# An MLP in fp16 pieces: how the largest magnitudes get to all partitions

## The chip, the cores and the metric

The kernel runs on one core of a Trainium2 chip. The metric is device microseconds of one execution. A core has five engines that work at the same time, each through its own queue in order: TensorE (PE, with its weight loads as PEld), VectorE (DVE), ScalarE (ACT), GpSimd (POOL) and SyncE (SP), which here issues nearly all DMAs. Engines wait for each other by semaphores. [...]

## The reference

The reference is one layer of a streaming encoder on x (1024 tokens by 1024, float32):

```
n    = RMSNorm(x) * norm1_g;  proj = n @ w_in      # columns: group A, group B
y    = concat(RMSNorm(attention_A(proj)), RMSNorm(attention_B(proj)))
h    = x + y @ w_out
n2   = RMSNorm(h) * norm2_g
u    = square(relu(n2 @ w_ff1))                    # 1024 x 4096
h    = h + u @ w_ff2
out  = RMSNorm(h) * final_norm_g
```

The change touches the MLP alone: the products with w_ff1 (1024 x 4096) and w_ff2 (4096 x 1024).

## The kernel before

The attention part takes the first 380 us or so and isn't touched. Behind it come three parts.

**Tail of the output projection (A).** out_proj_b(tb) makes 128 tokens of y @ w_out for group B on TensorE, for tb = 0 to 7; rows2(tb) adds the residual (VectorE, L1207), makes the row's norm and multiplies it in (L1218); first_half and second_half turn the rows by transposes (L172) and make sums of them for the MLP.

**First product (B).** w_ff1 is taken in eight blocks n of 512 columns. Each block is a matrix product in 2 x 2 sub-blocks by a scheme with seven products p instead of eight (Winograd's form of Strassen's), in the order 1, 5, 6, 3, 7, 2, 4. Each operand is the sum or difference of sub-blocks, and is held as two float16 pieces, a high one and a low one; a product of two such operands is three matmuls (mm3, recorded at L169 as all matmuls are). So a product p of a block is 24 matmuls of 128x128 by 128x512, and a block 168. product1(n, p) issues them; the PSUM results are added and kept by ScalarE (k, L1394) and VectorE (L1404), for p=4 also L1401 and L1402; then comes the squared ReLU on ScalarE (L1405, L1406) and, after p=4, four sums on VectorE (L1412 to L1418). put stores the seven operands for the second product in DRAM (ud).

So that float16 holds them, w is scaled by a power of two taken from its largest magnitude. This is the work that the change is about. For block n: load1(n) loads four tiles w (512 KB each); see1(n) reduces each tile to its largest magnitude per partition (VectorE, L1158); Top.send takes the largest of the four columns (L1163), writes this column of 128 numbers to DRAM (L1164), and reads it back as one row broadcast to all 128 partitions (all_w, L1166); scale1(n) reduces that row (topall, L1170), makes the powers of two (L1133 to L1140, L1312) and has ScalarE scale the four tiles in place (L1315). After that prepare1(n, p) makes the operand's sum (T, L1322, VectorE) and its two pieces: the high one on ScalarE (W, L1348), the low one on GpSimd (L1350), for a few on VectorE. It is called two products ahead of product1.

In the loop over (n, p), see1(n+1) is called after product p=6 of block n, and scale1(n+1) after p=7; for blocks 0 and 1 the calls lie in the loop over tb (scale1(0) after rows2(4), scale1(1) after rows2(7)).

**Second product (C and the end).** w_ff2 and u are taken in four groups g of two blocks, again seven products each, so 14 steps of 24 matmuls to a group. u comes back from ud (fetch2, three steps ahead), w by load2w; the operands are prepared by prepare2 (sums Z, L1322; pieces U and V, L1348 to L1352) two steps ahead; add_up adds a product to the accumulators (C, L1624, VectorE). One power of two per group for w (see2, scale2, with the same Top) and one for u (topu, filled at the end of product p=4 in the first product, and scale_of_u). For group g+1, w is loaded in steps 1 to 8 of group g and seen in steps 3 to 10, with the send after the last; scale2(g+1) is called in step 12. For group 0 all this lies in the last two blocks of the first product (scale2(0) after p=7 of block 7). scale_of_u(g) is called after p=5 of block 2g+2, for the last group in step 4 of group 0.

There are 16 such trips through DRAM: eight for w_ff1, four for w_ff2, four for u.

**What sets the order.** TensorE's instructions keep the order of the program text: each is tied to the one before it (pe, L134). The order of the other engines and of SP's DMAs is a planner's: it plays the program through with modelled durations and lets each engine take what its model has as ready, the earlier call first. So an instruction can stand well ahead of where it was written. Once planned, each engine keeps its order, and an instruction that waits holds up all behind it. SP's queue does so too: the read at L1166 waits there for the write at L1164 to land.

[...]

Of the kernel before, what the change touches and what calls it, by code (L numbers as in the profile page):

```python
# [17 lines left out]
P = 128  # L18
# [16 lines left out]
GQ = 2  # L35
# [21 lines left out]
def kernel(  # L57
# [113 lines left out]
    def transpose(*args):  # L171
        pe(nc.tensor.transpose(*args))  # L172
# [973 lines left out]
    class Top:  # L1146
# [10 lines left out]
        def see(self, src):  # L1157
            nc.vector.tensor_reduce(self.column(), flat(src), mybir.AxisListType.X, ALU.max, apply_absolute_value=True)  # L1158

        def send(self):  # L1160
            assert self.count == self.n
            top = small.tile([P, 1], F32, tag="top", bufs=3, name=f"top_{self.name}")
            nc.vector.tensor_reduce(top, self.cols[:, : self.n], mybir.AxisListType.X, ALU.max)  # L1163
            nc.sync.dma_start(tops[self.slot].rearrange("a p -> p a"), top)  # L1164
            self.all = small.tile([P, P], F32, tag="all", bufs=1, name=f"all_{self.name}")
            nc.sync.dma_start(self.all, tops[self.slot][0].partition_broadcast(P))  # L1166

# [132 lines left out]
    def see1(n, blocks=((0, 0), (0, 1), (1, 0), (1, 1))):  # L1300
        if n not in top1:
            top1[n] = Top(f"w1_{n}", n, 4)
        for b in blocks:
            top1[n].see(w1s[(n, *b)])
        if top1[n].count == 4:
            top1[n].send()

    def scale1(n):
        e = top1.pop(n).bits()
        up1 = power(scale_tile("up1", str(n), 2), e, -1.0, 254 + W_UP)  # L1310
        down1[n] = power(scale_tile("down1", str(n), 3), e, 1.0, -W_UP)
        nc.vector.tensor_tensor(down1[n], down1[n], xdown, ALU.mult)  # L1312
        for b in ((0, 0), (0, 1), (1, 1), (1, 0)):
            w = w1s[(n, *b)]
            nc.scalar.activation(w, w, AF.Copy, scale=up1)  # L1315
# [53 lines left out]
    def product1(n, p):  # L1369
        a, c = chains.setdefault(n, [None, None])  # L1370
        if p in (1, 5, 2):
            ps = pair_psum(f"f1_{n}_{p}")
            if p == 1:
                chains[n][0] = ps
            if p == 5:
                chains[n][1] = ps
        else:
            ps = c if p == 3 else a
        hi, lo = wops.pop((n, p))
        for u in range(2):  # L1380
            cols = slice(u * P, (u + 1) * P)
            for k in range(4):
                x2 = [X[p][k // 2][:, hl, k % 2] for hl in range(2)]
                mm3(ps[:, u], (hi[:, k, cols], lo[:, k, cols]), x2, k == 0 and p in (1, 5, 2), k == 3, True)
                if k % 2:
                    turn()
        kept = saved.setdefault(n, {})
        ps = flat(ps)
        if p in (1, 5, 6):
            if p == 5 and n:  # L1390
                kept[p] = tst([P, 2 * HALF], f"k{n}_{p}")
            else:
                kept[p] = page2([P, 2 * HALF], f"k{n}_{p}")
            nc.scalar.activation(kept[p], ps, AF.Copy)  # L1394
            return
        v = tst([P, 2 * HALF], f"v{n}") if p == 4 else kept[{3: 6, 7: 5, 2: 1}[p]]
        if n not in topf:
            topf[n] = small.tile([P, 4], F32, tag="topf", bufs=2, name=f"topf_{n}")
        top = topf[n][:, {3: 0, 7: 1, 2: 2, 4: 3}[p] :][:, :1]
        if p == 4:  # L1400
            nc.scalar.activation(v, ps, AF.Relu, scale=down1[n])  # L1401
            dve.tensor_reduce(top, ps, mybir.AxisListType.X, ALU.max)  # L1402
        else:
            dve.tensor_tensor_reduce(v, ps, v, 1.0, 0.0, ALU.add, ALU.max, top)  # L1404
            nc.scalar.activation(v, v, AF.Relu, scale=down1[n])  # L1405
        nc.scalar.activation(v, v, AF.Square)  # L1406
        if p != 4:
            put(n, {3: 2, 7: 4, 2: 1}[p], v)
            return

        u00, u01, u11, u10 = kept[1], kept[6], kept[5], v
        dve.tensor_tensor(u11, u10, u11, ALU.add)  # L1412
        put(n, 5, u11)
        dve.tensor_tensor(u10, u00, u10, ALU.subtract)
        put(n, 7, u10)
        dve.tensor_tensor(u00, u11, u00, ALU.subtract)
        put(n, 6, u00)
        dve.tensor_tensor(u01, u01, u00, ALU.subtract)  # L1418
        put(n, 3, u01)
        if n % GQ == 0:  # L1420
            topu[n // GQ] = Top(f"u{n // GQ}", NQ + n // GQ, GQ)
        top, col = topf.pop(n), topu[n // GQ].column()
        nc.vector.tensor_reduce(col, top, mybir.AxisListType.X, ALU.max)
        nc.vector.tensor_tensor(col, col, down1.pop(n), ALU.mult)
        if n % GQ == GQ - 1:
            topu[n // GQ].send()

    topf, topu = {}, {}

# [81 lines left out]
    def see2(g, tiles):  # L1511
        if g not in top2:
            top2[g] = Top(f"w2_{g}", NQ + NQ // GQ + g, 4 * GQ)
        for tile2 in tiles:
            top2[g].see(w2s[tile2])
        if top2[g].count == 4 * GQ:
            top2[g].send()

    def scale_of_u(g):
        e = topu.pop(g).bits(-10)  # L1520
        uup[g] = power(scale_tile("uup", str(g), 4), e, -2.0, 381 + U_UP)
        udown[g] = power(scale_tile("udown", str(g), 4), e, 2.0, -127 - U_UP)

    def scale2(g):
        e = top2.pop(g).bits(-30)
        up2[g] = power(scale_tile("up2", str(g), 2), e, -1.0, 254 + W_UP)
        down2[g] = power(scale_tile("down2", str(g), 2), e, 1.0, -W_UP)
        nc.vector.tensor_tensor(down2[g], down2[g], udown[g], ALU.mult)
# [17 lines left out]
    for at, (n, p) in enumerate(order1):  # L1546
        if p == (1 if n > 1 else 5) and n:
            load1(n + 1)
        ahead1 = at + (AHEAD1 + 1 if at < AT_ONCE else AHEAD1)

        behind = (n, p) == (0, 2)
        if ahead1 < len(order1) and not behind:
            prepare1(*order1[ahead1], ahead1)
        product1(n, p)
        for work in chores.get((n, p), ()):
            combined(*work)
            if behind and work[0] == 5:
                prepare1(*order1[ahead1], ahead1)
        if 0 < n < NQ - 1:
            if p == 6:  # L1560
                see1(n + 1)
            if p == 7:
                scale1(n + 1)
        if p == 5 and n and n % GQ == 0:
            scale_of_u(n // GQ - 1)
        if (n, p) in ((NQ - 2, 4), (NQ - 1, 1)):
            for tile2 in blocks2(0)[(p == 1) * 4 :][:4]:
                load2w(*tile2)
        if n == NQ - 1:
            if p in (5, 6):  # L1570
                see2(0, blocks2(0)[(p == 6) * 4 :][:4])
            if p == 6:
                for i in range(LOAD2):
                    fetch2(i)
            if p == 7:
                scale2(0)
            if p in (7, 2):
                prepare2({7: 0, 2: 1}[p])
# [113 lines left out]
    for at, (g, p, n) in enumerate(order2[:-GQ]):  # L1692
        fetch2(at + LOAD2)
        step = at % (7 * GQ)
        if g + 1 < NQ // GQ:
            if step in range(1, 9):
                load2w(*blocks2(g + 1)[step - 1])
            if step in range(3, 11):
                see2(g + 1, blocks2(g + 1)[step - 3 :][:1])
            if step == 12:  # L1700
                scale2(g + 1)
        if g + 1 == NQ // GQ and step == 0:
            down, up = down2[g], scale_tile("up", "", 1)
            nc.vector.reciprocal(up, down)
        if (g, step) == (0, 4):
            scale_of_u(NQ // GQ - 1)
        prepare2(at + AHEAD2)
        if at in (0, 1, 3, 5):
            load_acc(*into[{0: 1, 1: 5, 3: 6, 5: 4}[at]])
        if at == 6:  # L1710
            nc.sync.dma_start(gfb, final_g.partition_broadcast(P))
        if product2(g, p, n):
            for q2 in range(2):
                add_up(p, q2)
        if (g, p) == (NQ // GQ - 1, 3) and n % GQ == GQ - 1:
            gains.append(fps.tile([P, D], F32, tag=f"{'ab'[1 ^ g % 2]}0", bufs=1, name="gains"))
            nc.scalar.activation(gains[0], gfb, AF.Copy)
        if (g, p) == (NQ // GQ - 1, 7):
            if n % GQ == GQ - 1:
                h = acc[1, 0, 1][:, 1]  # L1720
                nc.vector.scalar_tensor_tensor(h, banks["a"][1][:, 1], down, h, ALU.mult, ALU.add)
            two = [final(2 * (n % GQ) + b, dve, nc.scalar) for b in range(2)]
            for _ in range(4):
                for work in two:
                    next(work)
# [106 lines left out]
```

## Time and profile before

| | |
|---|---|
| median of 3 runs | 1148.94 us (1145.35 to 1149.75) |
| the profiled execution: its time | 1152.16 us |
| the profiled execution: its span | 1150.1 us |
| TensorE busy, share of the span | 89% |
| VectorE | 67% |
| ScalarE | 57% |
| GpSimd | 35% |

The span runs from the first to the last instruction of the profiled execution; its time has a little more around it. Idle time of an engine costs nothing by itself: what counts is which wait ends last in a stage. In a row of the timeline stand start, duration, engine, line, operation and tiles, and in brackets the idle time before it with what ended it. In the waits stand, after the colon, the total in us, how often, and the longest. In the table of stretches, each engine has its busy us and its number of instructions; PEclk is the clock that TensorE was granted, as a share of the full one.

### The profile page before, as it was taken

The page shows a single profiled execution, that of the slowest core. Times are in us where ns is not written, and L with a number is a line of the kernel's source. Part 1 is how long each engine was busy: PE and PEld are TensorE (multiplying, and loading weights), DVE is VectorE, ACT ScalarE, POOL GpSimd, SP SyncE. Part 2 cuts the span into 40 slices and gives each one's busy share as a digit, 9 for nine tenths or more (in the row PEclk, how much of TensorE's full clock was granted, in tenths as well). Part 3 has the DMA queues.
Part 4 walks back from the last instruction along what each step waited for, and adds up shares of the span by engine and source line. Part 5 has one row for each costly group of instructions (what it writes and reads, how often), then busy time and mean ns, then how long its engine had stood idle before and what let it go on. Part 6 is the DMA issues. An engine that isn't in the chain of part 4 may idle for free.

```text
span 1150.1 us, 13982 instructions
## 1 busy us (share of the span) xinstructions
PE 1025.8 (89%) x4803; PEld 598.2 (52%) x4803; DVE 766.8 (67%) x1299; ACT 656.9 (57%) x1033; POOL 403.9 (35%) x327
## 2 busy tenths in 40 slices
PE   9999999999799785997987797969879979799997
PEld 7788878676567564443433343424324433344443
DVE  6577788776774455955564345326978968697976
ACT  8576676675767275755265355364734535356436
POOL 0566664334546231053344134233113014016023
PEclk9999999999899977998988989989989989999999
DMA  9843559999999531133443333455999345551003
GB/s 359 241 119 86 140 134 201 206 228 214 233 245 226 187 126 60 38 129 148 119 160 137 98 138 117 144 203 139 346 269 325 116 132 166 109 172 67 1 1 147
DMA packets 146183, 184.84 MB, mean 161 GB/s; under 512 B 80576, under 2 KB 100032, under 8 KB 146112
## 3 DMA queue, kind: packets, MB, share of 16 engines
q1 hardware_dynamic: 145968, 183.69, 55.5%
q8 instruction: 38, 0.62, 0.2%
q14 instruction: 33, 0.27, 0.1%
q10 hardware_dynamic: 144, 0.26, 0.1%
HBM read 104.21 MB, written 43.00 MB: 128 GB/s over the span
## 4 chain that ended last, share of the span: by engine, by line
PE 25%; DMA 22%; DVE 15%; issue 6%; ACT 6%; POOL 1%; SPq 0%; DVEq 0%; ACTq 0%; POOLq 0%
PE f L169 9%; DMA top<-top_w 5%; PE f_a L169 4%; DMA all_w<-top 4%; PE op_A L169 4%; DVE tops_w L1158 3%; DMA top<-top_u 3%; DMA w<-in_w_ff_dram 3%; PE f_c L169 3%; DMA u<-ud 3%; PE f_b L169 2%; DVE V L1352 2%; DVE C L1624 2%; ACT w L1315 2%; DVE Z L1322 1%
## 5 line engine op out<-in xcount | busy, mean ns | idle before, releaser
L169 PE MATMUL f<-X,W 128*128 128x512 f16 x1344 | 308.5, 394 | 47.4 <-DVE topf L1404 26.9
L169 PEld LDWEIGHTS <-W 128*128 128x128 f16 x1344 | 135.3, 101 | 219.6 <-issue 69.3
L169 PEld LDWEIGHTS <-U 128*128 128x128 f16 x1356 | 133.6, 99 | 194.7 <-issue 31.8
L169 PE MATMUL f_a<-V,U 128*128 128x512 f16 x756 | 169.7, 385 | 16.6 <-DVE C L1624 14.3
L1350 POOL TENSOR_TENSOR U<-u,U 128x1024 f16<-128x1024 f32 x32 | 76.2, 2388 | 244.0 <-ACT U L1348 200.9
L1350 POOL TENSOR_TENSOR W<-T,W 128x1024 f16<-128x1024 f32 x29 | 68.5, 2375 | 205.3 <-ACT W L1348 192.1
L169 PE MATMUL f_c<-V,U 128*128 128x512 f16 x384 | 87.6, 390 | 10.7 <-DVE C L1624 5.4
L1158 DVE TENSOR_REDUCE tops_w<-w 128x1 f32<-128x1024 f32 x64 | 75.9, 1212 | 29.2 <-DMA w<-in_w_ff_dram 29.1
L1346 ACT ACTIVATE u<-u,uup 128x1024 f32<-128x1024 f32 x32 | 36.4, 1144 | 59.0 <-DMA u<-ud 59.0
L1350 POOL TENSOR_TENSOR W<-w,W 128x1024 f16<-128x1024 f32 x23 | 52.2, 2271 | 46.5 <-ACT W L1348 46.5
L169 PE MATMUL op_A<-w_o,y 128*128 128x512 f32 x192 | 58.7, 433 | 8.3 <-DVE ts_vB L430 5.0
L617 ACT ACTIVATE P_B<-P_B,nm_B 128x640 f32<-128x640 f32 (+2 forms) x64 | 44.2, 691 | 29.7 <-DVE nm_B L614 15.3
L169 PE MATMUL op_B<-w_o,y 128*128 128x512 f32 x192 | 50.3, 417 | 10.5 <-DVE w_n L187 10.3
L1315 ACT ACTIVATE w<-w,up 128x1024 f32<-128x1024 f32 x32 | 34.1, 1136 | 44.5 <-DVE down L1140 43.3
L862 DVE SCALAR_TENSOR_TENSOR H_B<-P_B,rc_B,H_B 128x640 f16<-128x640 f32 (+2 forms) x64 | 51.7, 836 | 10.4 <-ACT H_B L857 10.2
L1348 ACT ACTIVATE V<-Z,up 128x1024 f16<-128x1024 f32 x32 | 36.4, 1139 | 33.2 <-DVE Z L1322 30.2
L169 PE MATMUL ip_qB<-nT,w_qB 128*128 128x512 f32 x192 | 53.8, 406 | 1.1 <-DVE t_kB L404 1.1
L169 PE MATMUL ip_kB<-nT,w_kB 128*128 128x512 f32 x192 | 53.7, 404 | 0.0
L1170 DVE TENSOR_REDUCE topall_w<-all_w 128x1 f32<-128x128 f32 x12 | 3.4, 286 | 73.9 <-DMA all_w<-top 73.9
L1394 ACT ACTIVATE k<-f 128x1024 f32<-128x1024 f32 x24 | 24.5, 1019 | 47.4 <-PE f L169 45.1
L169 PE MATMUL ip_vB<-nT,w_vB 128*128 128x512 f32 x192 | 51.2, 400 | 0.0
L1348 ACT ACTIVATE W<-T 128x1024 f16<-128x1024 f32 x32 | 33.4, 1049 | 31.2 <-DVE T L1322 27.4
(269 smaller groups left out, 2027.1 us busy)
## 6 DMA issues: line engine op xcount, KB each, us to landing
w<-in_w_ff_dram SPq DMA_DIRECT2D x64, 512.0 KB, 6.5
u<-ud SPq DMA_DIRECT2D x56, 512.0 KB, 6.1
ud<-k SPq DMA_DIRECT2D x48, 512.0 KB, 3.0
KkB<-t_kB SPq DMA_DIRECT2D x32, 256.0 KB, 5.1
xr<-in_x_dram SPq DMA_DIRECT2D x8, 512.0 KB, 8.8
st_o<-in_w_out_dram SPq DMA_DIRECT2D x8, 512.0 KB, 5.4
h<-in_x_dram SPq DMA_DIRECT2D x8, 512.0 KB, 4.8
hB<-h SPq DMA_DIRECT2D x8, 512.0 KB, 3.1
```

The source lines that it names most:

```text
L169: pe(nc.tensor.matmul(*args, **kw))
L617: nc.scalar.activation(pr, pr, AF.Exp, bias=nm, scale=-1.0, accum_out=sm)
L862: nc.vector.scalar_tensor_tensor(lo, q, rc, hi, ALU.mult, ALU.subtract)
L1158: nc.vector.tensor_reduce(self.column(), flat(src), mybir.AxisListType.X, ALU.max, apply_absolute_value=True)
L1315: nc.scalar.activation(w, w, AF.Copy, scale=up1)
L1322: engine.tensor_tensor(t, a, b, op)
L1346: nc.scalar.activation(full, full, AF.Copy, scale=up)
L1348: nc.scalar.activation(w[0], full, AF.Copy, scale=1.0 if up is None else up)
L1350: engine.tensor_tensor(w[1], full, w[0], ALU.subtract)
L1352: engine.scalar_tensor_tensor(w[1], full, up, w[0], ALU.mult, ALU.subtract)
L1394: nc.scalar.activation(kept[p], ps, AF.Copy)
L1624: nc.vector.scalar_tensor_tensor(flat(c), flat(ps), down2[g], flat(c), ALU.mult, ALU.add)
```

## The change

Top.send is cut into pieces. gather makes the column of 128 maxima as before. For the first product, spread turns that column, broadcast along the free axis, by one transpose on TensorE into a PSUM tile (tag tp), in which each partition has all 128 maxima; the reduce at L1170 then reads PSUM. This holds for all eight blocks of w_ff1, for u of groups 0 to 2, and for w_ff2 of group 0. The transpose is issued in scale1, scale_of_u and scale2, and so stands in TensorE's order at the place of these calls. For w_ff2 of groups 1 to 3 and for u of the last group, the trip through DRAM stays, but gather, write, read and use are separate calls. With it some calls move: see1(n+1) from p=6 to p=3, the product after it; scale2(0) from p=7 to p=3; load2w and see2 one step earlier, write in step 9, read in step 10, scale2(g+1) in step 12 as before; for the last u, write in step 1, read in step 2, use in step 5 of group 0.

```diff
@@ class Top
-        def send(self):
+        def gather(self):
             assert self.count == self.n
-            top = small.tile([P, 1], F32, tag="top", bufs=3, name=f"top_{self.name}")
-            nc.vector.tensor_reduce(top, self.cols[:, : self.n], mybir.AxisListType.X, ALU.max)
-            nc.sync.dma_start(tops[self.slot].rearrange("a p -> p a"), top)
+            self.top = small.tile([P, 1], F32, tag="top", bufs=3, name=f"top_{self.name}")
+            nc.vector.tensor_reduce(self.top, self.cols[:, : self.n], mybir.AxisListType.X, ALU.max)
+
+        def spread(self):
+            self.all = mps.tile([P, P], F32, tag="tp", bufs=2, name=f"all_{self.name}")
+            transpose(self.all, self.top.to_broadcast([P, P]), ident)
+
+        def write(self):
+            nc.sync.dma_start(tops[self.slot].rearrange("a p -> p a"), self.top)
+
+        def read(self):
             self.all = small.tile([P, P], F32, tag="all", bufs=1, name=f"all_{self.name}")
             nc.sync.dma_start(self.all, tops[self.slot][0].partition_broadcast(P))
@@ see1, product1, see2: send() becomes gather()
@@ scale1
     def scale1(n):
+        top1[n].spread()
         e = top1.pop(n).bits()
@@ scale_of_u, scale2
-    def scale_of_u(g):
+    def scale_of_u(g, spread=True):
+        if spread:
+            topu[g].spread()
         e = topu.pop(g).bits(-10)
...
     def scale2(g):
+        if g == 0:
+            top2[g].spread()
         e = top2.pop(g).bits(-30)
@@ the loop over the first product
         if 0 < n < NQ - 1:
-            if p == 6:
+            if p == 3:
                 see1(n + 1)
...
-            if p == 7:
+            if p == 3:
                 scale2(0)
@@ the loop over the second product
-            if step in range(1, 9):
-                load2w(*blocks2(g + 1)[step - 1])
-            if step in range(3, 11):
-                see2(g + 1, blocks2(g + 1)[step - 3 :][:1])
+            if step in range(8):
+                load2w(*blocks2(g + 1)[step])
+            if step in range(2, 10):
+                see2(g + 1, blocks2(g + 1)[step - 2 :][:1])
+            if step in (9, 10):
+                (top2[g + 1].write if step == 9 else top2[g + 1].read)()
             if step == 12:
                 scale2(g + 1)
...
-        if (g, step) == (0, 4):
-            scale_of_u(NQ // GQ - 1)
+        if g == 0 and step in (1, 2, 5):
+            last = NQ // GQ - 1
+            {1: topu[last].write, 2: topu[last].read, 5: lambda: scale_of_u(last, False)}[step]()
```

More of the change, by code (lines that the diff above doesn't have):

```diff
@@ L1305, in see1 @@
         if top1[n].count == 4:
-            top1[n].send()
+            top1[n].gather()
     def scale1(n):
+        top1[n].spread()
         e = top1.pop(n).bits()
@@ L1425, in product1 @@
         if n % GQ == GQ - 1:
-            topu[n // GQ].send()
+            topu[n // GQ].gather()
     topf, topu = {}, {}
@@ L1516, in see2 @@
         if top2[g].count == 4 * GQ:
-            top2[g].send()
-    def scale_of_u(g):
+            top2[g].gather()
+    def scale_of_u(g, spread=True):
+        if spread:
+            topu[g].spread()
         e = topu.pop(g).bits(-10)
```

## The prediction

> **What bounds the kernel now.** I read the page's shares first, then a table of stretches, then the waits, then single stalls in the timeline.
>
> ```profile
> span 1150.1 us, 13982 instructions
> PE 1025.8 (89%) x4803; PEld 598.2 (52%) x4803; DVE 766.8 (67%) x1299; ACT 656.9 (57%) x1033; POOL 403.9 (35%) x327
> ```
>
> TensorE is busy for most of the span, so the question is what its idle time is worth and where it lies. The table splits the span from the end of the output projection on: projection tail (A), first product (B), second product in two stretches (C), and a stretch for comparison.
>
> ```profile
> core 0: us, PE busy (x) PEld busy (x) DVE busy (x) ACT busy (x) POOL busy (x), PEclk, DMA share, GB/s
> 380.00:458.40 78.40, 52.88 (x240) 42.85 (x239) 39.56 (x89) 40.59 (x64) 15.73 (x14) 0.82 0.29 104
> 458.40:815.60 357.20, 309.83 (x1362) 137.06 (x1360) 195.40 (x273) 188.35 (x196) 119.87 (x52) 0.92 0.42 138
> 815.60:860.00 44.40, 36.12 (x153) 15.48 (x152) 36.56 (x37) 19.50 (x19) 5.33 (x2) 0.92 0.95 289
> 860.00:1010.00 150.00, 130.52 (x580) 56.96 (x578) 119.14 (x111) 70.39 (x67) 32.93 (x14) 0.95 0.58 173
> 1010.00:1102.00 92.00, 92.00 (x428) 41.66 (x426) 76.49 (x59) 48.13 (x46) 29.20 (x12) 1.00 0.20 69
> ```
>
> In the last row TensorE has no idle time and its full clock. Above it TensorE idles 25.5 us in A, 47.4 in B and 27.8 in C, and runs at a clock of 0.82 to 0.95. What it waits for stands in the waits; the second fence has the DMA queue's own.
>
> ```profile
> DVE topall_w L1170 <- DMA all_w<-top: 73.9, 12, 11.0
> ...
> DVE topall_u L1170 <- DMA all_u<-top: 41.6, 4, 11.4
> ...
> PE f L169 <- DVE topf L1404: 26.9, 5, 7.2
> ...
> PE f L169 <- ACT k L1394: 18.5, 2, 9.9
> ```
> ```profile
> SPq L1166 <- DMA top<-top_w: 56.8, 9, 7.4
> ...
> SPq L1166 <- DMA top<-top_u: 25.3, 4, 6.7
> ```
>
> VectorE stands still 115.5 us in 16 waits, each for the maximum's way through DRAM. TensorE never waits for that itself; it waits for VectorE and ScalarE work that is queued behind it. One stall (block n=4 of the first product) shows the chain, VectorE, ScalarE, GpSimd, TensorE:
>
> ```profile
> 653.36 0.29 DVE L1170 TENSOR_REDUCE topall_u<-all_u 128x1 f32<-128x128 f32 x1 [11.23 <-DMA all_u<-top]
> ...
> 656.74 0.28 DVE L1170 TENSOR_REDUCE topall_w<-all_w 128x1 f32<-128x128 f32 x1 [2.47 <-DMA all_w<-top]
> ```
> ```profile
> 657.68 4.27 ACT L1315 ACTIVATE w<-w,up 128x1024 f32<-128x1024 f32 x4 [12.59 <-DVE down L1140]
> 661.85 1.00 ACT L1394 ACTIVATE k<-f 128x1024 f32<-128x1024 f32 x1
> ```
> ```profile
> 663.93 2.13 POOL L1350 TENSOR_TENSOR W<-T,W 128x1024 f16<-128x1024 f32 x1 [17.51 <-ACT W L1348]
> 666.01 2.13 POOL L1350 TENSOR_TENSOR W<-w,W 128x1024 f16<-128x1024 f32 x1
> ```
> ```profile
> 662.90 49.65 PE L169 MATMUL f<-X,W 128*128 128x512 f16 x216 [8.51 <-ACT k L1394]
> ```
>
> VectorE idles 13.7 us for two trips, the scaling of w (L1315) starts only then, ScalarE's copy of a finished PSUM pair (k, L1394) is queued behind it, and TensorE idles 8.51 us for that PSUM pair.
>
> **The change, part by part.** The unit is the full-rate matmul, and the other prices are these:
>
> ```profile
> 1018.38 10.52 PE L169 MATMUL f_a<-V,U 128*128 128x512 f16 x48
> 1028.74 10.52 PE L169 MATMUL f_c<-V,U 128*128 128x512 f16 x48
> ```
> ```profile
> 24.08 0.60 PE L172 MATMUL r<-ident,r 128*128 128x128 f32 x4
> ...
> 407.44 0.41 PE L172 MATMUL tp<-ident,n 128*128 128x128 f32 x1
> ...
> 808.85 6.93 PE L169 MATMUL f<-X,W 128*128 128x512 f16 x24 [2.97 <-DVE topf L1404]
> ```
>
> From start to start 48 matmuls take 10.36 us, 0.216 each. After a gap of 2.97 us, 24 matmuls took 6.93 us where 5.18 is full rate: a gap costs itself and about 1.75 more. I use that for the clock lost per gap.
>
> *Spreading by TensorE (12 of the 16 maxima: 8 of w1, 3 of u, 1 of w2).* Added per maximum: one 128x128 transpose of a broadcast column. Four such cost 0.60 us, a lone one 0.41, so 0.15 to 0.41; I take 0.3, or 3.6 us in all, straight on TensorE, 0.6 of it in A and 3.0 in B. VectorE's reduce then reads PSUM in place of SBUF; I take the same 0.29. Removed: 24 small DMAs, and 12 of the queue's waits at L1166, during which everything behind them on SP (stores of k, loads of w and u) stood too. SP is not what TensorE waits for in A and B, so I book that at nothing; without that cover it is part of the range.
>
> *A, scale1(0) and scale1(1).*
>
> ```profile
> 400.81 0.29 DVE L1170 TENSOR_REDUCE topall_w<-all_w 128x1 f32<-128x128 f32 x1 [8.12 <-DMA all_w<-top]
> ...
> 446.33 0.28 DVE L1170 TENSOR_REDUCE topall_w<-all_w 128x1 f32<-128x128 f32 x1 [8.79 <-DMA all_w<-top]
> ```
> ```profile
> 404.75 2.90 PE L169 MATMUL op_B<-w_o,y 128*128 128x512 f32 x6 [10.32 <-DVE w_n L187]
> ...
> 455.74 1.12 PE L172 MATMUL tp<-ident,n 128*128 128x128 f32 x4 [12.22 <-ACT F L1263]
> ```
>
> Both large gaps of A end only after VectorE's two waits of 8.12 and 8.79. The new transposes stand behind out_proj_b(4) and out_proj_b(7) in TensorE's order, so VectorE has the rows' work (L1207, L1218) to do before them and waits for no trip. Gain: 8.1 + 8.8 = 16.9, plus two clocks of 1.75, less 0.6: 20. Bounds: 16 (no clock) to 28 (all 25.5 of idle, and clock).
>
> *B, six spreads in steady state and the three of u.* B holds 56 products of 24 matmuls; at full rate these 1344 are 1344 x 10.36 / 48 = 290.1 us; B takes 357.2, so 67.1 lie above it. What stays or comes: the 18 old transposes (1362 less 1344), 3; the new ones, 3; then two new dependences.
>
> First, TensorE now waits for the gathered column itself, and behind it in its strict order stand all later matmuls. The column was ready here (VectorE), against TensorE's place (product p=5 of n=2 ends 48 matmuls after 542.01, at 552.4):
>
> ```profile
> 519.51 0.15 DVE L1163 TENSOR_REDUCE top_w<-tops_w 128x1 f32<-128x4 f32 x1
> ...
> 545.80 1.22 DVE L1158 TENSOR_REDUCE tops_w<-w 128x1 f32<-128x1024 f32 x1 [4.16 <-DMA w<-in_w_ff_dram]
> ...
> 554.73 0.14 DVE L1163 TENSOR_REDUCE top_u<-tops_u 128x1 f32<-128x2 f32 x1
> ```
> ```profile
> 532.57 6.83 PE L169 MATMUL f<-X,W 128*128 128x512 f16 x24 [3.83 <-DVE topf L1404]
> ...
> 542.01 32.51 PE L169 MATMUL f<-X,W 128*128 128x512 f16 x142 [1.60 <-POOL W L1350]
> ```
>
> The first column of u would come 2.3 us late; that of w for n=2 comes early, since TensorE stopped at 528.7 after p=2, so p=7 ended near 523.5, 3.9 later. I book 3 us for the three of u and none for w.
>
> Second, scale1(n+1) can no longer start before p=7 of n has ended, and two products (10.4 us) later TensorE needs W(n+1, 1). In the stall shown the chain from the reduce (656.74) to the end of GpSimd's W<-w (668.14) takes 11.4. Ahead of W<-w in it stand W<-T (2.1 on GpSimd) and the copy of k (1.0), late there only because of the stall; without them it is 8.3, and with the transposes' 0.4 and one VectorE pass over 1024 columns before it (1.22, as at 545.80), 9.9: just hidden. Bounds: hidden, or 11.4 + 1.6 - 10.4 = 2.6 us idle per block. I take 1.0 x 7 blocks, 7, by the lower end, because nothing else should hold T back once VectorE runs; clock left over, 3. B gains 67.1 - 3 - 3 - 3 - 7 - 3 = 48; bounds 26 (2.6 x 7 idle with 1.75 x 7 of clock, and the rest) and 60.
>
> [...] The trace has the clock already lost after 2.97 us, so I keep a share.
>
> *C, see2 and load2w a step earlier, write, read and use apart.* Four trips stay (w2 of groups 1 to 3, the last u). VectorE's waits in C:
>
> ```profile
> 852.87 0.29 DVE L1170 TENSOR_REDUCE topall_u<-all_u 128x1 f32<-128x128 f32 x1 [7.77 <-DMA all_u<-top]
> ...
> 911.78 0.15 DVE L1163 TENSOR_REDUCE top_w<-tops_w 128x1 f32<-128x8 f32 x1
> ...
> 924.49 0.29 DVE L1170 TENSOR_REDUCE topall_w<-all_w 128x1 f32<-128x128 f32 x1 [6.65 <-DMA all_w<-top]
> ...
> 999.84 0.29 DVE L1170 TENSOR_REDUCE topall_w<-all_w 128x1 f32<-128x128 f32 x1 [7.52 <-DMA all_w<-top]
> ```
>
> A step is one product, 5.2 us. Gather to use was two steps (10.4), against a trip of 12.7 (911.78 to 924.49); now three (15.5), with SP's wait for the write moved behind a step's loads of u and w; the last u is written after one step, read after two and used after five instead of four. So a trip as measured is hidden, if the planner keeps to the written places: VectorE and SP are planned, and a read that the plan takes for ready can be drawn forward as before. The bound from the other engine: VectorE is busy 155.7 us in C's 194.4, and 733 matmuls need 158.2, so it can hardly fall below some 165. The three waits shown are worth up to 21.9 (the fourth trip was hidden behind other VectorE work); with the clock after three gaps, 5, up to 27. At worst, SP's queue moved past by earlier loads costs 5. I take half of the 27: 14.
>
> [...]
>
> Sum: 20 + 48 + 14 = 82. The profiled execution took 1152.16 us, 2.1 around its span and 3.2 above the median shown; taken off the median, 1148.9 - 82 = 1067.
>
> **Rivals.** *Everything hides*: A 28, B 58, C 24 give 1039. For it: each stall shown ends in one trip. Against: VectorE near its limit in C. *The trips of C still stall*, the planner having drawn them forward: 1067 + 14 = 1081. For it: the waits of 6.65 and 7.52 stood where two steps were written between. *The chain behind p=7 is the new bound*: 2.6 us and 1.75 of clock more per block take B to 26, and C's half goes with it when VectorE is late: 1149 - 20 - 26 - 3 = 1100. For it: 11.4 was measured; against: two of its parts came from the stall. *TensorE's own wait decides, slower*: a spread stands in strict order behind columns that wait for loads of w (4.16 us for one, four in a row for a block). It decides from 82 / 12 = 6.8 us per spread; at 8 us each, with 1.75 of clock, 117 come and 82 go: 1184. Against: the one late column above is late by 2.3. *Little comes of it* (the stalls pass to stores and loads on SP): 1130 to 1149.
>
> **How the numbers follow.** Forecast (1052 to 1076) 0.38; everything hides 0.17; trips of C still stall 0.13; chain 0.20; TensorE's wait, slower, 0.06; little 0.06, half of it within 0.5% (5.7 us, about what a measurement of this kernel can tell from no change). So faster 0.91, same 0.03, slower 0.06. The range goes from 1036 (all upper bounds but a little of C) to 1116 (the lower bounds 16 and 26, and a loss of some 9 in C).
>
> **What would show it.** VectorE's waits for all_w and all_u four, not sixteen; in A no gap of TensorE over 5 us and a clock above 0.9; in B, TensorE's waits on L1404 and L1394 (45.4 us) below 10, its idle time instead in front of the transposes or of W<-w; in C, VectorE's waits at L1170 below 11. It is wrong where the transposes themselves carry waits of 5 us and more, where B stays above 330 us, or where C does not shorten.

## The result and the profile after

The changed kernel takes 1087.68 us (median of 4 runs, 1085.46 to 1088.87); the kernel before, run beside it, 1147.91 (4 runs, 1145.35 to 1149.75). The ratio is 0.9475, with a 95% interval of 0.9449 to 0.95: some 60 us less, where 82 were forecast. The time lies in the range, and 21 us above the predicted one.

The profiled execution took 1085.46 us. The page's shares of the kernel after:

```profile
span 1083.7 us, 13981 instructions
...
PE 1013.8 (94%) x4815; PEld 594.1 (55%) x4815; DVE 790.1 (73%) x1299; ACT 652.2 (60%) x1033; POOL 402.2 (37%) x327
```

The same work of TensorE lies in a span that is 66.4 us shorter (the medians differ by 60.2: the execution that was profiled before lay 4.2 above its median, the one after 2.2 below). The table of stretches of the kernel after, cut at the same places of the work as the prediction's table:

```profile
core 0: us, PE busy (x) PEld busy (x) DVE busy (x) ACT busy (x) POOL busy (x), PEclk, DMA share, GB/s
380.00:433.60 53.60, 48.73 (x237) 39.65 (x236) 39.39 (x79) 31.45 (x53) 14.44 (x12) 0.97 0.37 135
433.60:752.40 318.80, 301.46 (x1371) 135.67 (x1371) 217.70 (x285) 191.66 (x203) 119.52 (x52) 0.98 0.43 152
752.40:796.40 44.00, 38.45 (x168) 16.58 (x166) 40.85 (x41) 20.25 (x20) 5.19 (x2) 0.92 0.91 316
796.40:943.40 147.00, 128.08 (x565) 55.89 (x564) 114.17 (x105) 69.79 (x66) 32.86 (x14) 0.94 0.51 169
```

A fell from 78.4 to 53.6 us and its clock rose from 0.82 to 0.97; B fell from 357.2 to 318.8, clock 0.92 to 0.98. C is what it was: 44.4 and 150.0 us before, 44.0 and 147.0 now, at clocks of 0.92 and 0.95 before, 0.92 and 0.94 now. Measured from the first matmul of op_B (which itself comes 1.1 us earlier) to the first of f, from there to the first of f_a, and from there to the end of the span, the three parts give the span's difference whole:

| us | before | after | gain | forecast |
|---|---|---|---|---|
| up to op_B | 376.0 | 374.9 | 1.1 | 0 |
| A | 82.5 | 58.7 | 23.8 | 20 |
| B | 357.1 | 318.9 | 38.2 | 48 |
| C and the end | 334.5 | 331.2 | 3.3 | 14 |

In the waits of the kernel after, first VectorE's on the trip, then TensorE's in B and C (total, how often, longest):

```profile
DVE topall_w L1178 <- DMA all_w<-top: 18.2, 2, 9.3
```
```profile
PE f_a L169 <- DVE C L1637: 13.6, 5, 7.0
PE all_u L172 <- DVE top_w L1163: 5.7, 2, 2.8
...
PE f_c L169 <- DVE up L1140: 4.2, 1, 4.2
PE all_u L172 <- DVE top_u L1163: 4.0, 1, 4.0
...
PE f L169 <- POOL W L1359: 2.8, 3, 1.2
```

The 45.4 us that TensorE waited in B for topf and k are gone. In their place stand three waits of the new transposes of u (all_u, 9.7 us) and three for W<-w (2.8). In C nothing went away. VectorE's timeline there, with SP's queue, for one of the three trips of w2 left:

```profile
840.57 0.15 DVE L1163 TENSOR_REDUCE top_w<-tops_w 128x1 f32<-128x8 f32 x1
...
853.55 0.29 DVE L1178 TENSOR_REDUCE topall_w<-all_w 128x1 f32<-128x128 f32 x1 [9.31 <-DMA all_w<-top]
...
856.20 1.28 DVE L1637 SCALAR_TENSOR_TENSOR C<-f_a,down,C 128x1024 f32<-128x1024 f32 x1
...
929.47 0.29 DVE L1178 TENSOR_REDUCE topall_w<-all_w 128x1 f32<-128x128 f32 x1 [8.92 <-DMA all_w<-top]
```
```profile
840.75 0.32 SPq L1170 DMA_DIRECT2D top<-top_w  x1
847.80 0.32 SPq L1174 DMA_DIRECT2D all_w<-top  x1
848.21 0.86 SPq L1492 DMA_DIRECT2D u<-ud  x2
```

The read is written a step (5.2 us) behind the write, with that step's loads between; in SP's queue it stands right behind the write, waits 7 us for it to land, and holds the loads of u up. The reduce is written three steps (15.5 us) behind the gather; in VectorE's order three passes stand between, and then it waits 9.31 us of the trip's 13.0. Before, such a wait was 6.65. So both were drawn forward, as the planner does with what its model has as ready.

### The profile page after: what moved, and what is told of

The parts are those of the page before. It is cut to its first block, busy times and chain, and to the rows that moved or that the text cites. A ratio compares the mean times of both kernels' runs of the same rounds, so it can differ in the third digit from the quotient of the medians.

```text
span 1083.7 us, 13981 instructions
## 1 busy us (share of the span) xinstructions
PE 1013.8 (94%) x4815; PEld 594.1 (55%) x4815; DVE 790.1 (73%) x1299; ACT 652.2 (60%) x1033; POOL 402.2 (37%) x327
## 4 chain that ended last, share of the span: by engine, by line
PE 28%; DVE 19%; DMA 9%; ACT 9%; issue 6%; POOL 2%; SPq 0%; DVEq 0%; ACTq 0%; POOLq 0%
PE f L169 9%; PE f_a L169 6%; DMA w<-in_w_ff_dram 4%; PE op_A L169 4%; DVE tops_w L1158 3%; PE f_c L169 3%; DVE V L1361 3%; ACT w L1324 2%; PE op_B L169 2%; PE f_b L169 2%; DVE C L1637 2%; DMA u<-ud 2%; DVE T L1331 2%; DVE Z L1331 1%; DMA top<-top_w 1%
## 5 line engine op out<-in xcount | busy, mean ns | idle before, releaser
L169 PE MATMUL f<-X,W 128*128 128x512 f16 x1344 | 299.3, 385 | 3.5 <-POOL W L1359 2.8
L169 PEld LDWEIGHTS <-W 128*128 128x128 f16 x1344 | 133.0, 99 | 166.0 <-issue 9.8
L1359 POOL TENSOR_TENSOR W<-T,W 128x1024 f16<-128x1024 f32 x29 | 65.4, 2266 | 104.3 <-ACT W L1357 99.7
L1403 ACT ACTIVATE k<-f 128x1024 f32<-128x1024 f32 x24 | 24.4, 1018 | 49.6 <-PE f L169 49.5
L1413 DVE CUSTOM_DVE_ANT_0 k<-f,k 128x1024 f32<-128x1024 f32 x24 | 29.2, 1219 | 34.4 <-PE f L169 34.2
L1414 ACT ACTIVATE k<-k,down 128x1024 f32<-128x1024 f32 x24 | 27.4, 1142 | 41.1 <-DVE topf L1413 41.0
L1357 ACT ACTIVATE U<-u,uup 128x1024 f16<-128x1024 f32 x24 | 27.4, 1141 | 38.8 <-DMA u<-ud 15.5
L169 PE MATMUL ip_qA<-nT,w_qA 128*128 128x512 f32 x192 | 50.2, 395 | 0.3 <-DVE VA L175 0.3
```

The lines of the kernel that those rows point to most:

```text
L169: pe(nc.tensor.matmul(*args, **kw))
L1357: nc.scalar.activation(w[0], full, AF.Copy, scale=1.0 if up is None else up)
L1359: engine.tensor_tensor(w[1], full, w[0], ALU.subtract)
```

## The experiments

The runs were made in two sets, on two chips; the kernel before had a median of 1147.52 us (13 runs) beside the first four kernels, and of 1151.18 (7 runs) beside the others, so kernels of different sets are compared by their ratios to it. The first set holds only_first, only_second, pin_use and u_later, the second dram_pinned, pin_use_read, u_pin and u_pin_see.

### The spreading by TensorE alone (only_first)

The second product's loop is put back; the 12 transposes stay.

```diff
-            if step in range(8):
-                load2w(*blocks2(g + 1)[step])
...
+            if step in range(1, 9):
+                load2w(*blocks2(g + 1)[step - 1])
+            if step in range(3, 11):
+                see2(g + 1, blocks2(g + 1)[step - 3 :][:1])
+            if step == 10:
+                top2[g + 1].write()
+                top2[g + 1].read()
...
+        if (g, step) == (0, 4):
+            scale_of_u(NQ // GQ - 1, False)
```

> The changed kernel with its second product put back: for w_ff2 of groups 1 to 3 load, see and send stand at their old steps, write and read together, and the last u is written and read where it is gathered and used in step 4. Theory (the three steps that lie apart are worth next to nothing, because the plan draws read and use forward in any case): 1088 us, within 5 of the changed kernel, VectorE's waits for all_w and all_u in the second product some 20 us as in both kernels. Rival (the second product gained about what the forecast gave it, and the first product less than thought): 1095 to 1105 us.

Measured: 1090.18 us, ratio 0.9505 (0.9478 to 0.9532), against 0.9475 (0.9449 to 0.95) with both parts. By the spans A is 58.5, B 319.2, C and the end 334.6. So the transposes carry the gain, and the second part adds 3.4 us in C by the spans, an amount that the intervals of the times hardly tell from nothing. VectorE's timeline of this kernel has the same trips in C:

```profile
795.92 0.29 DVE L1178 TENSOR_REDUCE topall_u<-all_u 128x1 f32<-128x128 f32 x1 [7.39 <-DMA all_u<-top]
...
865.54 0.29 DVE L1178 TENSOR_REDUCE topall_w<-all_w 128x1 f32<-128x128 f32 x1 [6.21 <-DMA all_w<-top]
...
939.67 0.29 DVE L1178 TENSOR_REDUCE topall_w<-all_w 128x1 f32<-128x128 f32 x1 [8.16 <-DMA all_w<-top]
```

They come to 21.8 us against 20.9 with the steps apart (2.69 for u, 9.31 and 8.92 for w): what the second part took off the wait for u, it gave back on w.

### The steps apart alone (only_second)

In the first product each spread becomes a write and a read right behind the gather, and see1 and scale2(0) go back to p=6 and p=7; the second product stays as changed.

```diff
             top1[n].gather()
+            top1[n].write()
+            top1[n].read()
...
-        top1[n].spread()
         e = top1.pop(n).bits()
...
-            if p == 3:
+            if p == 6:
                 see1(n + 1)
```

> The kernel before with the second product's part of the change alone: the first product's maxima go through DRAM as before. Theory: the gain belongs to TensorE's spreading, so 1142 to 1150 us, with VectorE's twelve waits of 6 to 11 us back in the first product. Rival (the second product's steps carry 10 to 15 us): 1132 to 1138 us.

Measured: 1145.91 us, ratio 0.9991 (0.9973 to 1.001). Alone, the second part is worth nothing that can be measured. B is 356.6, as before; C with the end is 332.1, about as after; VectorE's waits for the trips are back, 114.1 us in 15.

### The reduce tied behind the last add (pin_use)

If C stalls because the reduce is drawn forward, a tie between two VectorE instructions should be enough: the reduce may stand no earlier in VectorE's order than the add_up last written before it. Trip, DMAs and written places stay.

```diff
-            nc.vector.tensor_reduce(top, self.all, mybir.AxisListType.X, ALU.max)
+            behind_of(nc.vector.tensor_reduce(top, self.all, mybir.AxisListType.X, ALU.max), behind)
...
-        e = topu.pop(g).bits(-10)
+        e = topu.pop(g).bits(-10, last_add[0])
...
-        e = top2.pop(g).bits(-30)
+        e = top2.pop(g).bits(-30, last_add[0])
...
-        nc.vector.scalar_tensor_tensor(flat(c), flat(ps), down2[g], flat(c), ALU.mult, ALU.add)
+        last_add[0] = nc.vector.scalar_tensor_tensor(flat(c), flat(ps), down2[g], flat(c), ALU.mult, ALU.add).ins.name
```

> The changed kernel; in the second product VectorE's reduce of the broadcast maxima is tied, in VectorE's order, behind the last add_up written ahead of it, so that it can't be drawn forward. Theory (the trips of the second product still stall VectorE for 9.3 and 8.9 us since the plan draws the reduce forward): those two waits go below 3 us each, TensorE's gaps of 4.2 and 7.0 us near 857 and 931 go, 1070 to 1078 us. Rival (VectorE is near its limit there, so that another wait takes their place): 1084 to 1092 us.

Measured: 1078.13 us, ratio 0.9402 (0.937 to 0.9433): 9.6 less than the changed kernel, 0.1 above the theory's range and well below the rival's. C and the end fall from 331.2 to 322.1; A and B stay (58.3 and 318.6). VectorE's timeline has two of the reduces, each with its gather ahead of it:

```profile
798.80 0.15 DVE L1169 TENSOR_REDUCE top_w<-tops_w 128x1 f32<-128x8 f32 x1
...
828.76 2.47 DVE L1644 SCALAR_TENSOR_TENSOR C<-f_b,down,C 128x1024 f32<-128x1024 f32 x2
831.14 0.28 DVE L1184 TENSOR_REDUCE topall_w<-all_w 128x1 f32<-128x128 f32 x1
...
848.19 0.14 DVE L1169 TENSOR_REDUCE top_w<-tops_w 128x1 f32<-128x8 f32 x1
...
906.50 2.47 DVE L1644 SCALAR_TENSOR_TENSOR C<-f_b,down,C 128x1024 f32<-128x1024 f32 x2
908.88 0.28 DVE L1184 TENSOR_REDUCE topall_w<-all_w 128x1 f32<-128x128 f32 x1
```

Neither waits; VectorE has no wait for a trip left. So the place of the use in VectorE's order was what failed. The three written steps (15.5 us) are not what hides the trip here: the gather is still drawn forward while its use no longer is, and 32.3 and 60.7 us lie between the two. Without VectorE's 20.9 us of waits TensorE's idle time in C falls from 31.6 to 24.4 us, and its busy time from 299.7 to 297.8 (the mean granted clock of the whole execution is 0.981 against 0.975); 17.4 us of what is left are waits for the adds to C.

### The read's place on SP too (pin_use_read)

As pin_use, and the read on SP is tied behind the load of u last written before it.

```diff
-            nc.sync.dma_start(self.all, tops[self.slot][0].partition_broadcast(P))
+            behind_of(nc.sync.dma_start(self.all, tops[self.slot][0].partition_broadcast(P)), last_fetch[0])
...
-        nc.sync.dma_start(u2s[n, p], ud[n][p - 1])
+        last_fetch[0] = nc.sync.dma_start(u2s[n, p], ud[n][p - 1]).ins.name
```

> pin_use, with the read of the row in SP's queue tied behind the load of u issued last before it, so that fewer loads of u stand behind SP's wait for the write to land. Theory (once VectorE no longer waits, SP's 7 us in front of the read don't reach TensorE): within 3 us of pin_use. Rival (the loads of u behind the read are what is left of the stall): 4 to 8 us below pin_use.

Measured: 1078.22 us, ratio 0.9365 (0.9335 to 0.9395) against 0.9402 (0.937 to 0.9433), spans 1074.0 against 1073.0, C and the end 321.9 against 322.1. But the tie moved nothing. SP's queue at the same trip, first in pin_use, then with the tie:

```profile
848.36 0.32 SPq L1176 DMA_DIRECT2D top<-top_w  x1
849.55 0.32 SPq L1498 DMA_DIRECT2D u<-ud  x1
856.02 0.32 SPq L1180 DMA_DIRECT2D all_w<-top  x1
```
```profile
850.58 0.32 SPq L1178 DMA_DIRECT2D top<-top_w  x1
851.77 0.32 SPq L1501 DMA_DIRECT2D u<-ud  x1
858.90 0.32 SPq L1182 DMA_DIRECT2D all_w<-top  x1
```

In pin_use a load of u already stood between write and read, and all through C the order of SP's DMAs is the same in both kernels. So this is pin_use once more, on the other chip: it shows that C repeats to 0.2 us, and that the ratios of one order can lie 0.4% apart, some 4 us. Whether the loads of u that stand behind the read cost anything stays open.

### The scale of u one product later (u_later)

The three waits of the all_u transposes are the other loss. In the changed kernel scale_of_u(g) is called at p=5 of the next block; here at p=6, one product (5.2 us) later in TensorE's order. Nothing else differs.

```diff
-        if p == 5 and n and n % GQ == 0:
+        if p == 6 and n and n % GQ == 0:
             scale_of_u(n // GQ - 1)
```

> The changed kernel; scale_of_u of groups 0 to 2, and with it the transpose that TensorE waits in, is called after product p=6 in place of p=5, one product (5.2 us) later. Theory (TensorE waits at the three transposes of u, 2.8, 2.8 and 4.0 us, for a column that is gathered behind a reduce that waits for a load of w; the gaps and the clock after them are lost time): no wait left at these transposes, 1072 to 1078 us. Rival (the wait only moves to the next thing that is late): 1084 to 1090 us.

Measured: 1070.79 us, ratio 0.9332 (0.9305 to 0.936): 16.9 less than the changed kernel, 13.8 by the spans, and below the 1072 to 1078 that the theory gave. B falls from 318.9 to 303.7; C with the end is 331.0 (331.2). A is 60.5 (58.7) here and 58.6 in u_pin below, which has the same edit: a part can differ by some 2 us between two executions. The first of the three in TensorE's timeline, after the change and with the call a product later:

```profile
529.89 0.32 PE L172 MATMUL all_u<-ident,top_u 128*128 128x128 f32 x1 [2.83 <-DVE top_w L1163]
530.05 17.39 PE L169 MATMUL f<-X,W 128*128 128x512 f16 x72
547.28 0.27 PE L172 MATMUL all_w<-ident,top_w 128*128 128x128 f32 x1
547.38 36.46 PE L169 MATMUL f<-X,W 128*128 128x512 f16 x168
...
583.79 10.96 PE L169 MATMUL f<-X,W 128*128 128x512 f16 x50
```
```profile
533.83 0.27 PE L172 MATMUL all_u<-ident,top_u 128*128 128x128 f32 x1
533.94 10.52 PE L169 MATMUL f<-X,W 128*128 128x512 f16 x48
```

The transpose no longer waits, and the 48 matmuls behind it run at full rate (10.36 us from 533.94 to the next transpose at 544.30). (The view puts the wait of 2.83 down to top_w, a column that VectorE gathers right behind top_u, at 529.76; the transpose reads top_u.) After the wait of 2.83, the 72 matmuls from 530.05 to 547.28 took 17.2 us, where full rate is 15.5: 1.7 of clock, beside the wait. Behind the second wait, of 2.83 too, 72 matmuls took 17.2 us again, and behind the third, of 4.00, 17.0. The three places make 9.7 + 1.7 + 1.7 + 1.5 = 14.6; the run gives 15.2.

### Trips through DRAM, but used late (dram_pinned)

How much of the first part is the shorter way, and how much the place of its use? Here all 16 maxima go through DRAM again, written and read right behind the gather, but the reduce is tied behind VectorE's last pass over PSUM written before it (in A, behind the rows' multiplication by the norm). scale_of_u and scale2(0) are called at p=7. Each of the three kinds of maxima of the first product has its own all tile.

```diff
             top1[n].gather()
+            top1[n].write()
+            top1[n].read()
...
-        top1[n].spread()
-        e = top1.pop(n).bits()
+        e = top1.pop(n).bits(-90, last_pass[0])
...
-            dve.tensor_tensor_reduce(v, ps, v, 1.0, 0.0, ALU.add, ALU.max, top)
+            last_pass[0] = dve.tensor_tensor_reduce(v, ps, v, 1.0, 0.0, ALU.add, ALU.max, top).ins.name
```

> The changed kernel with the first product's maxima sent through DRAM again, written and read as soon as they are gathered; VectorE's reduce of the row that comes back is tied, in VectorE's order, behind the last pass of product p=7 (for the two blocks ahead of the loop behind the last row multiply), so that it can't be drawn forward; the scales of u are taken at p=7 as well, that of w_ff2 of group 0 too. Theory A (what cost the time was the place of the reduce in VectorE's order, which the transpose only sets by TensorE's order): the trips lie in the slack of 13 to 30 us between gather and p=7, waits are left where the slack is short (block 2, 4 us, w_ff2 of group 0), 1085 to 1105 us. Theory B (the way over TensorE counts because it is short): the waits of 6 to 11 us stay, 1130 to 1150 us.

Measured: 1101.57 us, ratio 0.956 (0.9537 to 0.9582). A is 60.4 (82.5 before, 58.7 after), B 327.2 (357.1, 318.9), C and the end 334.9. So with the old way through DRAM, 22 of A's 24 us and 30 of B's 38 are there. From its VectorE timeline, and TensorE's:

```profile
518.67 0.29 DVE L1188 TENSOR_REDUCE topall_w<-all_w 128x1 f32<-128x128 f32 x1 [5.49 <-DMA all_w<-top]
...
594.78 1.22 DVE L1166 TENSOR_REDUCE tops_w<-w 128x1 f32<-128x1024 f32 x1 [9.15 <-DMA w<-in_w_ff_dram]
```
```profile
525.76 1.03 PE L169 MATMUL f<-X,W 128*128 128x512 f16 x2 [4.82 <-ACT W L1368]
...
606.55 0.98 PE L169 MATMUL f<-X,W 128*128 128x512 f16 x2 [2.87 <-ACT W L1368]
```

Of the first product's twelve reduces one still waits for its trip (5.49), and TensorE then for W (4.82). Its other waits for trips, 22.0 us in three, lie in C, which isn't tied here. VectorE waits longer for a load of w than in the changed kernel (9.15 us against at most 5.5); SP issued a load of w at 586.26, right behind a read (584.88) that had waited for its write. This kernel has u's scale late too, so for the way itself it is to be set beside u_later: A 60.4 against 60.5, B 327.2 against 303.7. Of the 75 us that u_later has gained in A and B, 52 are there without crossing by TensorE, and 23.5 come with it, all in B. How these divide among the trip that still waits, the loads behind SP's reads and the clock wasn't separated. In A, where see1 is called at the places it had before, the 22 us are the tie's, as far as the edit goes. In B they aren't the tie's alone: see1(n+1) stays at p=3, so that the gather is called earlier than in the kernel before, u's scale is taken at p=7, and the all tiles are separate. No run has the tie there without these.

### Both repairs together (u_pin), and the reduces of w2 tied as well (u_pin_see)

u_pin has the edits of pin_use and u_later.

> pin_use and u_later together. Theory (two stalls in two stages, each with its own cause): the gains add up, 1087.7 - 9.6 - 16.9 = 1061 us. Rival (both take from the same slack): 1066 us or more.

Measured: 1063.36 us, ratio 0.9237 (0.9222 to 0.9251). The two gains, 9.6 and 16.9 off 1087.68, make 1061.2; by the ratios they make 0.9402 + 0.9332 - 0.9475 = 0.9259. So they add, as they lie in different parts: B is 303.6, C and the end 324.9. What then holds TensorE in C is late adds: 17.5 us in eight waits for C. see2's reduces over w2 (1.2 us each, some waiting for their load) are drawn in front of them, so u_pin_see ties those too:

```diff
-            top2[g].see(w2s[tile2])
+            top2[g].see(w2s[tile2], last_add[0])
```

> u_pin, with the reduces of w_ff2's tiles (see2) tied behind the last add_up as well. Theory (at the start of the second product TensorE waits 5 us for add_up of the first products, which stands in VectorE's order behind reduces for the next group that could come later): the gap near the third product goes, 1054 to 1058 us. Rival (VectorE is full there, and the order among its work makes no difference, or the late reduces make the write late): 1060 to 1066 us.

Measured: 1053.61 us, ratio 0.915 (0.9136 to 0.9164), a little below the theory's range, 8.5% below the kernel before and 3.4% below the changed one (0.915 / 0.9475). C and the end fall to 315.0. VectorE's timeline, and TensorE's at the same time:

```profile
803.41 1.28 DVE L1644 SCALAR_TENSOR_TENSOR C<-f_b,down,C 128x1024 f32<-128x1024 f32 x1 [1.02 <-PE f_b L169]
806.00 1.28 DVE L1644 SCALAR_TENSOR_TENSOR C<-f_b,down,C 128x1024 f32<-128x1024 f32 x1 [1.30 <-PE f_b L169]
815.37 0.29 DVE L1184 TENSOR_REDUCE topall_w<-all_w 128x1 f32<-128x128 f32 x1 [8.08 <-DMA all_w<-top]
```
```profile
805.80 10.52 PE L169 MATMUL f_a<-V,U 128*128 128x512 f16 x48
817.51 0.38 PE L169 MATMUL f_a<-V,U 128*128 128x512 f16 x1 [1.19 <-ACT V L1363]
818.86 10.30 PE L169 MATMUL f_a<-V,U 128*128 128x512 f16 x47 [0.97 <-DVE V L1367]
```

VectorE waits for trips again, 16.4 us in three waits, 8.08 of it in this one, against 18.2 in two for w in the changed kernel: now that the gather is held back too, VectorE comes to the reduce 7 to 9 us behind it, and the trips take 15.5, 13.1 and 12.0. But the adds stand ahead of the wait: behind this one TensorE idles 1.19 and 0.97 us, behind the 9.31 of the changed kernel 4.21. What a wait costs is what stands behind it.

## Why the prediction was right, and where not

*The bound.* Right: the gain came from VectorE's waits for the trips and what was queued behind them. dram_pinned makes it sharper than the prediction had it: some two thirds of what u_later gains in A and B (52 of 75 us) can be had with the old way through DRAM, if the reduce stands late in VectorE's order and, in B, the gather is called early. In A that is 22 of the changed kernel's 24 us, so there the transposes gain by the place that they give the reduce, through TensorE's strict order, and hardly by being a shorter way; in B place and way weren't separated further.

*A, 20 forecast, 23.8 measured.* Right, within its bounds of 16 to 28. Both gaps of 10.32 and 12.22 us are gone, and no gap over 2.3 us stays in A; the clock is 0.97. The idle time in the stretch fell from 25.5 to 4.9 us (53.6 less 48.73), by 20.6, where the two waits had been booked at 16.9; what the smaller gaps lost as well was left out of the forecast.

*B, 48 forecast, 38.2 measured.* The mechanism was right, and the terms for what comes in its place were mis-sized. The step that failed is "I book 3 us for the three of u and none for w". None for w held: the longest wait of a transpose of w is 0.21 us. For u the prediction took one column's lateness, 2.3, for the sum of three, without clock. The three columns made TensorE wait 2.83, 2.83 and 4.00 and cost 15 with the clock, as u_later shows. This is the mechanism of the rival "TensorE's own wait decides": VectorE's timeline has the wait for a load of w ahead of the column,

```profile
520.62 1.22 DVE L1158 TENSOR_REDUCE tops_w<-w 128x1 f32<-128x1024 f32 x1 [4.04 <-DMA w<-in_w_ff_dram]
...
529.69 0.14 DVE L1163 TENSOR_REDUCE top_u<-tops_u 128x1 f32<-128x2 f32 x1
```

and TensorE's transpose at 529.89 directly behind it. No run takes that load's wait away by itself, so its share in the lateness is read from the rows. The rival's mechanism struck three spreads, at 5 us each with the clock, not twelve at 8, so it took a part of the gain and not the sign.

Two other terms of B were booked too high and made up some of it. The chain behind p=7, booked 7, cost 2.8: only three of the waits for W<-w are left, of at most 1.2 us, so the rival that put it at 1100 is out. The new transposes, booked at 0.3 each, take 0.15: from 547.38 to 583.79, 168 matmuls and one transpose took 36.41, where 168 at full rate are 36.26.

One term was missing: in front of the last old transposes, near B's start, TensorE now waits 2.24 us for F of ScalarE (445.97) and 1.92 for S of VectorE (448.54), where it had no wait before. So 12 us more for u and 4 for these, less 4 for the chain and 1.5 for ten new transposes, make some 10, about the 9.8 that B fell short. (The prediction's lower bound of 26 for B comes to between 24.6 and 27.6 by its own terms; this moves neither the forecast nor the range by more than 2 us.)

*C, 14 forecast, 3.3 measured.* Wrong. The step was "a trip as measured is hidden, if the planner keeps to the written places", taken at half. It doesn't keep to them, which the prediction named and priced: the rival "the trips of C still stall" is what happened in C. only_second shows the part alone at nothing, and pin_use that 9.1 us of the 14 were there to be had, with one tie. Whether three written steps would hide a trip was never seen: VectorE came to the reduce 3.7 us behind the gather in the changed kernel's row, 32 and 61 us behind it in pin_use's two, and 7 to 9 in u_pin_see. By its own sign, then, that part was wrong: C hardly shortened, and VectorE's waits for the trips were 20.9 us, not below 11.

*The sum.* 82 less 66.4 by the spans is 15.6 too much: 9.8 in B and 10.7 in C, less 3.8 and 1.1 that A and the part before op_B gave. The rest of the 21 us lies in the executions that were profiled, 6.2, less the 1.0 by which the kernel before ran faster beside this one than in the runs the prediction started from.

## What to carry to other kernels

In an engine that keeps its order, a wait for a DMA costs what stands behind it (here 4.21 us of TensorE's time for a wait of 9.31, and 1.19 and 0.97 for one of 8.08): before shortening the way, look in the timeline at where the waiting instruction stands, and move or tie it behind the work that others need. Where a planner sets the order, a greater distance in the program text is no distance in the queue until a dependence makes it one (three written steps left VectorE 20.9 us of waits, one tie none); and a dependence that the planner's order keeps already moves nothing (321.9 us for C and the end against 322.1), so compare the queue with and without it. Where a strictly ordered engine takes over the wait (here TensorE's transposes), check the lateness of each producer by itself, and give each gap its clock: one product later was worth 14 to 17 us here.

## What the runs showed of the hardware that was not expected

**The clock after a short gap.** The stretches behind TensorE's gap of 2.83 us in the changed kernel, and in the last two rows those behind its gap of 1.19 us at 516.96:

```profile
core 0: us, PE busy (x) PEld busy (x) DVE busy (x) ACT busy (x) POOL busy (x), PEclk, DMA share, GB/s
530.05:533.50 3.45, 3.45 (x12) 1.40 (x11) 3.35 (x5) 0.00 (x0) 1.70 (x1) 0.65 0.37 152
533.50:537.00 3.50, 3.50 (x16) 1.47 (x14) 1.29 (x3) 0.00 (x0) 0.00 (x0) 0.86 0.58 210
537.00:547.00 10.00, 10.00 (x48) 4.51 (x47) 1.23 (x2) 4.17 (x4) 2.13 (x1) 1.00 0.12 42
...
517.00:520.00 3.00, 3.00 (x15) 1.35 (x16) 0.00 (x0) 3.00 (x4) 3.00 (x2) 1.00 0.55 168
520.00:527.00 7.00, 7.00 (x33) 3.04 (x31) 6.38 (x8) 4.06 (x5) 3.62 (x3) 1.00 0.39 155
```

The granted clock is 0.65 and 0.86 for the 7 us behind the longer gap, then 1.00; behind the shorter it is 1.00 throughout. 3.45 x 0.35 + 3.5 x 0.14 = 1.7 us, the loss found from the matmuls. So this gap of 2.83 us cost clock, and the one of 1.19 did not, where the prediction had taken 1.75 us per gap. The length alone doesn't settle it: in pin_use the gaps in front of the same three transposes are 2.82, 2.83 and 3.81 us, and the 72 matmuls behind them took 15.5 us (529.01 to 544.55), 17.2 (605.87 to 623.09) and 18.4 (685.54 to 703.95), which is 0, 1.7 and 2.9 more than at full rate. What else decides, no run here shows.

**A trip of a 512-byte column.** In the changed kernel 13.0 us pass from the column (840.57) to its use (853.55): 7.05 from the write's issue until the read goes out behind it (840.75 to 847.80), and 5.75 more until the reduce of what was read (64 KB, the row on all partitions). Over the kernel's three trips of w the medians from issue to landing are 7.1 us for the write (0.5 KB) and 5.7 for the read. What of it is the traffic, and what the way through SP, no run here separates.
